# Moving the row sums of the modulation vectors to other gates

## The chip, the cores and the metric

The kernel runs on one core of one Trainium2 chip. The metric is the time of one execution on the device in microseconds (us), as the median of several runs. The kernel before takes 2740.04 us (three runs, 2739.88 to 2740.99).

The engines appear under the short names of the profile: PE is TensorE (matmuls), PEld its weight loads, DVE is VectorE, ACT is ScalarE, POOL is GpSimd, and SP is SyncE, whose queue issues nearly all DMA transfers here. Each engine works through its own list of instructions in a fixed order and waits for the others by semaphores.

## The reference

The reference runs two blocks on 256 tokens of width 1024. Only the first block matters here. It has two trunk layers; layer 0 works on two streams, `lat` and `ctx`, layer 1 on `lat` alone at its end. Each layer begins with modulation vectors, six of width 1024 per stream, from one linear map of a condition:

```python
m_lat = (jax.nn.silu(c) @ w_mod + b_mod)[:, None, :]
m_ctx = jax.nn.silu(c_ctx) @ w_mod + b_mod
sh1, sc1, g1, sh2, sc2, g2 = jnp.split(m_lat, N_MOD, -1)
...
u_lat = h_lat * (1.0 + sc1) + sh1
y_lat, y_ctx = token_mixers(u_lat, u_ctx, ...)
h_lat = layer_norm(DN_ALPHA * h_lat + g1 * y_lat, ln1_g, ln1_b)
u_lat = h_lat * (1.0 + sc2) + sh2
h_lat = layer_norm(DN_ALPHA * h_lat + g2 * expert_choice_ffn(u_lat, ...), ln2_g, ln2_b)
```

The token mixers are four branches (A: global attention, B: Fourier, C: window attention, D: neighbourhood attention). Each branch is multiplied with a matrix and with a gate, a sigmoid of another product of `u`, and the four are added up:

```python
gates = jax.nn.sigmoid(gate_logits)
merged = gates[..., :D_MODEL] * (branches[0] @ w_branch[0])
for i in range(1, N_BRANCH):
    merged = merged + gates[..., i * D_MODEL:(i + 1) * D_MODEL] * (branches[i] @ w_branch[i])
return merged @ w_out
```

## The kernel before

**Matmuls from split weights.** A weight tile of 1 MB (`raw`, 128 x 2048 floats) is loaded by one DMA on SP's queue. Each half of it is split into a high part `wh` on ACT (L257) and a low part `wl` on DVE (L260), and each product is three matmuls (L294 high by high, L295 the one that needs `wl`, L296). `dense_nat` (L298) goes over the tiles of a product and behind each half of a tile calls `pump(1)`.

**Slots.** `raw` tiles take slots in turn: three in the mixers of layer 0, five in those of layer 1. A load waits until the tile that held its slot before, three (five) tiles earlier in the program, has been read.

**Gates.** `gate(i, c)` (L710) handles half `c` of the columns of branch `i`; the text calls it gate 00, 01, 10 and so on. It multiplies `u` with two gate tiles (`wgat`) for every unit of 128 tokens (four units in layer 0, two in layer 1), takes tanh of the result on ACT (`th`), multiplies the split branch (`brs`, split in L272 and L273) with half a branch tile (`wbr`), and combines both on DVE: L737 for branch 0, else L739 into `th`, and an addition into `mg` on POOL (L740; on DVE for the last branch). A gate's products lie in four banks (`acc`) that must be read out before the next ones use them. The order of the steps in the program is written out: `A al ac B F C cl cc 00 01 10 11 D dl dc 20 21 30 31`, where a capital letter is a projection and `al`, `cl`, `dl` (`ac`, ...) are attentions of `lat` (`ctx`). A list scheduler then orders each engine's instructions by priority and its own estimate of when inputs are there; PE fills the wait times of an attention with matmuls of the gate behind it.

**Row sums.** The first third of layer 0's modulation comes from matmuls at the start. The rest, two thirds for layer 0 and three for layer 1, comes from DVE. `mods_rows(l, i, n)` (L486) makes eight steps for a third `i` of layer `l` and `n` streams. A step loads a 1 MB tile of the transposed matrix (`wmt`), and for each half and stream multiplies it with the row of silu(c) (`crow`) and adds up along the row (L497, output `junk` and one column of `mcol`): 2n instructions. The last step of eight adds the bias (L502). They are issued 100 places later in priority, behind the last `wl` split. The steps wait in the list `todo`; `pump(n)` (L507) runs the next n of them, if there are any.

**Who calls pump.** Before each pair of gates, `hook(i)` fills `todo` with the eight steps of one third: (0,1) for two streams with branch 0, (0,2) for two with branch 1, (1,0) for two with branch 2, (1,1) for one with branch 3; in layer 1, (1,2) for one with branch 0. The loop that matters:

```python
                for hi, lo in parts:
...
                    for u, (xh, xl, o) in enumerate(units):
...
                    kg += kp
                    self.pump(1)
```

Of the kernel before, what the change touches and what calls it, by code (L numbers as in the profile page):

```python
# [190 lines left out]
class Net:  # L191
# [99 lines left out]
    def mm3(self, out, xs, ws, first, last):  # L291
        (xh, xl), (wh, wl) = xs, ws
        mm = self.nc.tensor.matmul
        mm(out, lhsT=xh, rhs=wh, start=first, stop=False)  # L294
        mm(out, lhsT=xh, rhs=wl, start=False, stop=False)  # L295
        mm(out, lhsT=xl, rhs=wh, start=False, stop=last)  # L296
# [315 lines left out]
    def mixers(self, mg, gp, pool, l, streams, with_ctx, hook):  # L612
# [16 lines left out]
        nf = len(full)  # L629
# [46 lines left out]
        def who(ss, u):  # L676
            return ss[u // 2], u % 2
# [32 lines left out]
        def gate(i, c):  # L710
            if c == 0:
                hook(i)
            th = {}

            def evac_g(_, u, acc):
                x = gp.tile([128, 512], F32, tag="th", name="th", bufs=(3, 4)[nf - 1])
                th[u] = x
                nc.scalar.activation(x, acc, AF.Tanh, scale=0.5)

            self.dense_nat(us, [[wg[2 * i + c, 0], wg[2 * i + c, 1]]], evac_g)  # L720
            wb = gp.tile([128, 1024], F32, tag="wbr", name="wbr", bufs=1)
            nc.sync.dma_start(wb, I[f"wbr{l}"][i][:, c * 1024:(c + 1) * 1024])
            if c == 0:
                for s in full:
                    brs[s] = self.new_split(gp, 2, 256, "brs" + s)
                    self.split_x(brs[s], br[i, s])
            hi, lo = self.split_w(wb)[0]
            hi, lo = (x.rearrange("p (k n) -> p k n", k=2) for x in (hi, lo))
            for u in range(len(us)):
                s, t = who(full, u)  # L730
                acc = self.bank("acc")
                o = slice(t * 128, (t + 1) * 128)
                for k in range(2):
                    self.mm3(acc, (brs[s][0][:, k, o], brs[s][1][:, k, o]), (hi[:, k], lo[:, k]), k == 0, k == 1)
                m = mg[s, t][:, c * 512:(c + 1) * 512]
                if i == 0:
                    nc.vector.scalar_tensor_tensor(m, th[u], 1.0, acc, op0=OP.add, op1=OP.mult)  # L737
                else:
                    nc.vector.scalar_tensor_tensor(th[u], th[u], 1.0, acc, op0=OP.add, op1=OP.mult)  # L739
                    (nc.gpsimd if i < 3 else nc.vector).tensor_tensor(m, m, th[u], op=OP.add)  # L740
            self.pump(8 if c else 0)


        A = new_mixer()
# [122 lines left out]
        for i in range(4):  # L867
            for c in range(2):
                steps[f"{i}{c}"] = lambda i=i, c=c: gate(i, c)
# [683 lines left out]
    def first(self):  # L1553
# [6 lines left out]
        for l in range(2):  # L1560
            full = names if l == 0 else names[:1]
            post = ExitStack()
            with ExitStack() as sc:
# [27 lines left out]
                    with self.later(400), self.tc.issue_after(self.last_split.ins):  # L1591
                        self.residual(z["lat"], I["ln2_g0"], I["ln2_b0"])

                todo = ([(0, 1, 2)], [(0, 2, 2)], [(1, 0, 2)], [(1, 1, 1)]) if l == 0 else ([(1, 2, 1)], [], [], [])

                def hook(i):
                    self.todo = [f for a in todo[i] for f in self.mods_rows(*a)]

                mr = xsc.enter_context(tc.tile_pool(name="mr", bufs=1))
                n = 2 - l  # L1600
# [9 lines left out]
                with tc.tile_pool(name=f"gate{l}", bufs=1) as gp, tc.tile_pool(name=f"mix{l}", bufs=1) as pool:  # L1610
                    self.ahead = ahead
                    self.mixers(mg, gp, pool, l, xt, l == 0, hook)
# [201 lines left out]
```

## Time and profile before

| what | us |
|---|---|
| median of the timed runs (2739.88 to 2740.99) | 2740.04 |
| the profiled execution, its own time | 2735.72 |
| span of the profiled execution, first to last instruction | 2733.9 |
| TensorE busy in the span | 2431.8 |
| VectorE busy in the span | 1473.5 |
| ScalarE busy in the span | 849.0 |

The mixers of layer 0 run from about 60 to 450 us, their gates from 135 us; then come the output product, the router and the experts of layer 0, and from 1030 us layer 1, whose gates run from about 1090 to 1272 us. A row of the timeline gives the start in us, the duration in us, engine, line, operation, the tiles written and read with their shapes, and a count; in square brackets stands how long the engine was idle just before, and what it waited for. A matmul of the timeline reads as 0.39 us although the next starts 0.23 us later, since they are pipelined. A row of the stage table gives a stretch, its length, and then busy us and number of instructions of PE, PEld, DVE, ACT and POOL, then the granted clock as a share of the full one, the share of the DMA engines and GB/s.

### The profile page before, as it was taken

What the parts mean: (1) busy time and instruction counts of PE and PEld (TensorE: products, weight loads), DVE (VectorE), ACT (ScalarE), POOL (GpSimd) and SP (SyncE); (2) the same over time, 40 slices, a digit from 0 to 9 for tenths busy, and PEclk for the clock granted to TensorE, in tenths of its full rate; (3) what the DMA queues carried; (4) which work ended last, traced back from release to release, by engine and by line L of the source; (5) the groups of instructions that cost most, each with busy time, mean ns of one, the idle gap of its engine ahead of it and who ended that gap; (6) DMA issues with size and microseconds to landing.
All of it is one profiled execution on the core that took longest, in us unless ns stands there. A gap on an engine that the chain in (4) does not pass through costs nothing.

```text
span 2733.9 us, 34804 instructions
## 1 busy us (share of the span) xinstructions
PE 2431.8 (89%) x13994; PEld 1662.4 (61%) x13994; DVE 1473.5 (54%) x2601; ACT 849.0 (31%) x1442; POOL 88.8 (3%) x89
## 2 busy tenths in 40 slices
PE   6999899898898988999856777689999999998998
PEld 3667678552222227668511333369778998877897
DVE  4799896442222238866411212169656755656655
ACT  2443233220000014544100100036454544544543
POOL 0001010000000000010000000000000000000000
PEclk8999999999998899999977877889999999999999
DMA  8146565489999993646899999974264652543650
GB/s 295 37 147 219 157 226 210 152 332 407 421 421 421 422 372 128 225 135 231 333 426 426 426 425 426 426 272 155 93 221 176 253 186 89 193 175 145 234 186 31
DMA packets 116384, 700.83 MB, mean 256 GB/s; under 512 B 26352, under 2 KB 27120, under 8 KB 34688
## 3 DMA queue, kind: packets, MB, share of 16 engines
q1 hardware_dynamic: 114304, 692.33, 65.2%
q0 software_dynamic: 1920, 6.29, 0.6%
q8 instruction: 110, 1.80, 0.3%
q14 instruction: 50, 0.41, 0.0%
HBM read 693.33 MB, written 5.24 MB: 256 GB/s over the span
## 4 chain that ended last, share of the span: by engine, by line
PE 66%; DMA 17%; DVE 11%; ACT 3%; issue 2%; POOL 1%; SPq 0%; DVEq 0%; ACTq 0%; POOLq 0%
PE acc L295 9%; PE acc L296 9%; PE acc L294 9%; PE acc L1018 9%; DMA raw<-in_wgu 6%; PE acc L1050 5%; DMA raw<-in_wdn 3%; PE att L368 2%; PE att L369 2%; DMA raw<-in_xwv 2%; PE att L370 2%; DVE wl L260 2%; PE tp L378 2%; PE att L985 2%; PE acc L369 2%
## 5 line engine op out<-in xcount | busy, mean ns | idle before, releaser
L260 DVE TENSOR_TENSOR wl<-raw,wh 128x1024 fp32r<-128x1024 f32 x384 | 471.0, 1233 | 283.8 <-ACT wh L257 279.0
L257 ACT ACTIVATE wh<-raw 128x1024 fp32r<-128x1024 f32 x384 | 403.7, 1058 | 558.5 <-PE acc L296 258.0
L1018 PE MATMUL acc<-raw,xs 128*64 128x512 f32 (+1 forms) x2048 | 379.1, 647 | 60.6 <-DMA raw<-in_wgu 60.4
L1018 PEld LDWEIGHTS acc<-raw,xs 128*64 128x64 f32 (+1 forms) x2048 | 99.4, 126 | 308.8 <-issue 181.6
L1022 ACT ACTIVATE eth<-acc 64x512 f32<-64x512 f32 x48 | 28.4, 591 | 670.6 <-PE acc L1018 670.6
L1024 DVE SCALAR_TENSOR_TENSOR esg<-eth,acc 64x512 f32<-64x512 f32 x48 | 32.7, 681 | 353.3 <-ACT eth L1022 352.8
L294 PE MATMUL acc<-wh,xtlath 128*128 128x512 f32 (+1 forms) x448 | 177.4, 397 | 8.8 <-ACT wh L257 3.2
L295 PE MATMUL acc<-wl,xtlath 128*128 128x512 f32 (+1 forms) x448 | 176.7, 394 | 2.7 <-DVE wl L260 2.7
L296 PE MATMUL acc<-wh,xtlatl 128*128 128x512 f32 (+1 forms) x448 | 175.9, 393 | 0.0
L497 DVE SCALAR_TENSOR_TENSOR junk<-raw,crow 128x1024 bf16<-128x1024 f32 x128 | 162.2, 1267 | 8.6 <-DMA raw<-in_wmt 7.2
L1050 PE MATMUL acc<-raw,eaT 128*64 128x512 f32 x512 | 140.2, 710 | 10.3 <-DVE eaT L207 5.5
L368 PE MATMUL att<-xth,wh 128*128 128x256 f32 x512 | 146.2, 286 | 2.9 <-DVE xth L288 2.9
L369 PE MATMUL att<-xth,wl 128*128 128x256 f32 x512 | 146.0, 285 | 0.0
L370 PE MATMUL att<-xtl,wh 128*128 128x256 f32 x512 | 145.8, 285 | 0.0
L368 PE MATMUL acc<-xth,wh 128*128 128x256 f32 x416 | 120.3, 289 | 4.5 <-DVE xth L288 4.5
L369 PE MATMUL acc<-xth,wl 128*128 128x256 f32 x416 | 120.0, 289 | 0.0
L370 PE MATMUL acc<-xtl,wh 128*128 128x256 f32 x416 | 119.4, 287 | 0.0
L294 PEld LDWEIGHTS acc<-wh,xtlath 128*128 128x128 f32 x448 | 85.5, 191 | 29.0 <-ACT wh L257 3.8
L1061 DVE TENSOR_TENSOR eylat<-acc,g2lat 32x512 f32<-32x512 f32 x32 | 21.9, 684 | 150.3 <-PE acc L1050 150.1
L294 PE MATMUL acc<-wh,xtctxh 128*128 128x512 f32 (+1 forms) x272 | 101.8, 375 | 1.0 <-DVE th L739 1.0
L368 PEld LDWEIGHTS att<-xth,wh 128*128 128x128 f32 x512 | 99.5, 194 | 3.8 <-issue 3.2
L294 PE MATMUL acc<-wh,hidh 128*128 128x512 f32 x256 | 101.3, 396 | 0.0
(535 smaller groups left out, 4844.7 us busy)
## 6 DMA issues: line engine op xcount, KB each, us to landing
raw<-in_wgu SPq DMA_DIRECT2D x256, 1024.0 KB, 19.5
raw<-in_wdn SPq DMA_DIRECT2D x128, 1024.0 KB, 19.0
raw<-in_w SPq DMA_DIRECT2D x64, 1024.0 KB, 4.8
raw<-in_wmt SPq DMA_DIRECT2D x40, 1024.0 KB, 4.9
raw<-in_wgat SPq DMA_DIRECT2D x32, 1024.0 KB, 4.8
raw<-in_wmod SPq DMA_DIRECT2D x8, 1024.0 KB, 7.5
raw<-in_wqkv SPq DMA_DIRECT2D x8, 1024.0 KB, 10.7
wbr<-in_wbr SPq DMA_DIRECT2D x16, 512.0 KB, 4.8
```

What stands on the lines that cost most here:

```text
L257: self.nc.scalar.activation(hi, s, AF.Copy)
L260: self.last_lo = self.nc.vector.tensor_tensor(lo, s, hi.bitcast(F32), op=OP.subtract)
L294: mm(out, lhsT=xh, rhs=wh, start=first, stop=False)
L295: mm(out, lhsT=xh, rhs=wl, start=False, stop=False)
L296: mm(out, lhsT=xl, rhs=wh, start=False, stop=last)
L368: mm(acc[:, b], lhsT=h[:, s], rhs=xh[:, k], start=k == 0, stop=False)
L369: mm(acc[:, b], lhsT=l[:, s], rhs=xh[:, k], start=False, stop=False)
L370: mm(acc[:, b], lhsT=h[:, s], rhs=xl[:, k], start=False, stop=k == 7)
L378: self.nc.tensor.transpose(t[:, j], src[:, (b + j) * 128:(b + j + 1) * 128], self.ident)
L497: nc.vector.scalar_tensor_tensor(junk, r[:, b * 1024:b * 1024 + 1024], 1.0, self.crow[:, s], op0=OP.mult, op1=OP.mult, accum_out=self.mcol ...
L1018: nc.tensor.matmul(o, lhsT=lt, rhs=w[:, a, c], start=k == 0, stop=k == 7)
L1050: nc.tensor.matmul(yb[64 * h:64 * h + 64], lhsT=aT[:, kf], rhs=w[:, f, h * 512:(h + 1) * 512], start=kf == 0, stop=kf == 7)
```

## The change

The last line of `gate` and the filling of `todo` are edited. All thirds of a layer go into `todo` at once, at the first gate: three in layer 0, two in layer 1. The third (1,1) moves from layer 0 to layer 1. The last line of a gate now runs `nf - 1` steps (`nf` is the number of streams, 2 in layer 0 and 1 in layer 1), and at the very last gate whatever is left.

```diff
-            self.pump(8 if c else 0)
+            self.pump(len(self.todo) if i == 3 and c else nf - 1)
...
-                todo = ([(0, 1, 2)], [(0, 2, 2)], [(1, 0, 2)], [(1, 1, 1)]) if l == 0 else ([(1, 2, 1)], [], [], [])
+                todo = ((0, 1, 2), (0, 2, 2), (1, 0, 2)) if l == 0 else ((1, 1, 1), (1, 2, 1))
...
                 def hook(i):
-                    self.todo = [f for a in todo[i] for f in self.mods_rows(*a)]
+                    if i == 0:
+                        self.todo = [f for a in todo for f in self.mods_rows(*a)]
```

The first place is DVE's queue in layer 0 at the start of gate 10. Numbers behind names only tell tiles apart. Before, from the branch tile's split of gate 01 (`wl_1866`) to the two splits of gate 10's first tile (`wl_1908`, `wl_1912`):

```order
L260 TENSOR_TENSOR wl_1866<-wbr_1863,wh_1865 128x1024
L497 SCALAR_TENSOR_TENSOR junk_1777,mcol0_83<-raw_1775,crow_226 128x1024 x4
L260 TENSOR_TENSOR wl_1908<-raw_1905,wh_1907 128x1024
L497 SCALAR_TENSOR_TENSOR junk_1818,mcol0_83<-raw_1816,crow_226 128x1024 x4
L737 SCALAR_TENSOR_TENSOR mg_152<-th_1855,acc_1869 128x512
L737 SCALAR_TENSOR_TENSOR mg_153<-th_1857,acc_1877 128x512
L260 TENSOR_TENSOR wl_1912<-raw_1905,wh_1911 128x1024
```

In the changed kernel the same two splits are `wl_1922` and `wl_1926`:

```order
L737 SCALAR_TENSOR_TENSOR mg_155<-th_1868,acc_1900 128x512
L497 SCALAR_TENSOR_TENSOR junk_1825,mcol0_83<-raw_1823,crow_226 128x1024
L273 TENSOR_TENSOR brslatl_2074<-br_972,brslath_2073 128x512
L497 SCALAR_TENSOR_TENSOR junk_1825,mcol0_83<-raw_1823,crow_226 128x1024
L273 TENSOR_TENSOR brsctxl_2078<-br_991,brsctxh_2077 128x512
L502 TENSOR_TENSOR mcol0_83<-mcol0_83,bmodt_81 128x32
L497 SCALAR_TENSOR_TENSOR junk_1857,mcol0_83<-raw_1855,crow_226 128x1024 x4
L497 SCALAR_TENSOR_TENSOR junk_1910,mcol0_83<-raw_1908,crow_226 128x1024
L260 TENSOR_TENSOR wl_1922<-raw_1919,wh_1921 128x1024
L260 TENSOR_TENSOR wl_1926<-raw_1919,wh_1925 128x1024
```

Counted from the start of the program, 24 row sums stood ahead of the first of these splits before, and 37 stand ahead of it now. They also stood on either side of the last combinations of gate 01 (`mg`), and now stand behind them.

The second place is DVE's queue in layer 0 at the projection D. Before, the end of the gate's row sums and the splits of D's second tile (`raw_2368`):

```order
L497 SCALAR_TENSOR_TENSOR junk_2219,mcol0_83<-raw_2217,crow_226 128x1024
L273 TENSOR_TENSOR brslatl_2979<-br_1166,brslath_2978 128x512
L497 SCALAR_TENSOR_TENSOR junk_2219,mcol0_83<-raw_2217,crow_226 128x1024
L273 TENSOR_TENSOR brsctxl_2983<-br_1351,brsctxh_2982 128x512
L497 SCALAR_TENSOR_TENSOR junk_2250,mcol0_83<-raw_2248,crow_226 128x1024 x4
L502 TENSOR_TENSOR mcol0_83<-mcol0_83,bmodt_81 128x32
L260 TENSOR_TENSOR wl_2371<-raw_2368,wh_2370 128x1024
L260 TENSOR_TENSOR wl_2375<-raw_2368,wh_2374 128x1024
```

In the changed kernel, the splits of both of D's tiles (`raw_2338` and `raw_2396`):

```order
L497 SCALAR_TENSOR_TENSOR junk_2272,mcol1_84<-raw_2270,crow_226 128x1024
L273 TENSOR_TENSOR brslatl_3008<-br_1166,brslath_3007 128x512
L497 SCALAR_TENSOR_TENSOR junk_2272,mcol1_84<-raw_2270,crow_226 128x1024
L273 TENSOR_TENSOR brsctxl_3012<-br_1351,brsctxh_3011 128x512
L497 SCALAR_TENSOR_TENSOR junk_2272,mcol1_84<-raw_2270,crow_226 128x1024 x2
L260 TENSOR_TENSOR wl_2341<-raw_2338,wh_2340 128x1024
L260 TENSOR_TENSOR wl_2345<-raw_2338,wh_2344 128x1024
L497 SCALAR_TENSOR_TENSOR junk_2329,mcol1_84<-raw_2327,crow_226 128x1024 x4
L260 TENSOR_TENSOR wl_2399<-raw_2396,wh_2398 128x1024
L260 TENSOR_TENSOR wl_2403<-raw_2396,wh_2402 128x1024
```

Before, the splits of D's first tile stood behind 53 and 57 row sums and those of the second behind 64. Now both splits of the first stand behind 76, and those of the second behind 80.

The third place is DVE's queue in layer 1, in gate 01. Before, the splits of its two gate tiles (`raw_7602`, `raw_7636`):

```order
L260 TENSOR_TENSOR wl_7605<-raw_7602,wh_7604 128x1024
L207 COPY PT_7272<-tp_7347 128x4x128
L260 TENSOR_TENSOR wl_7609<-raw_7602,wh_7608 128x1024
L260 TENSOR_TENSOR wl_7639<-raw_7636,wh_7638 128x1024
L273 TENSOR_TENSOR brslatl_7677<-br_7003,brslath_7676 128x512
L497 SCALAR_TENSOR_TENSOR junk_7553,mcol1_84<-raw_7551,crow_6478 128x1024
L1639 TENSOR_SCALAR resg_8622<-g_8580 128x8
L1639 TENSOR_SCALAR resb_8623<-b_8582 128x8
L497 SCALAR_TENSOR_TENSOR junk_7570,mcol1_84<-raw_7568,crow_6478 128x1024
L260 TENSOR_TENSOR wl_7643<-raw_7636,wh_7642 128x1024
```

In the changed kernel these tiles are `raw_7561` and `raw_7605`:

```order
L260 TENSOR_TENSOR wl_7568<-raw_7561,wh_7567 128x1024
L497 SCALAR_TENSOR_TENSOR junk_7512,mcol1_84<-raw_7510,crow_6437 128x1024
L273 TENSOR_TENSOR brslatl_7656<-br_6962,brslath_7655 128x512
L497 SCALAR_TENSOR_TENSOR junk_7529,mcol1_84<-raw_7527,crow_6437 128x1024
L1640 TENSOR_SCALAR resg_8622<-g_8580 128x8
L1640 TENSOR_SCALAR resb_8623<-b_8582 128x8
L497 SCALAR_TENSOR_TENSOR junk_7529,mcol1_84<-raw_7527,crow_6437 128x1024
L502 TENSOR_TENSOR mcol1_84<-mcol1_84,bmodt_81 128x16
L497 SCALAR_TENSOR_TENSOR junk_7585,mcol1_84<-raw_7583,crow_6437 128x1024 x2
L497 SCALAR_TENSOR_TENSOR junk_7602,mcol1_84<-raw_7600,crow_6437 128x1024 x2
L260 TENSOR_TENSOR wl_7608<-raw_7605,wh_7607 128x1024
L260 TENSOR_TENSOR wl_7612<-raw_7605,wh_7611 128x1024
```

The split that directly followed the first tile's pair now has seven row sums ahead of it. PE's order stays that of before except for a few places where matmuls that need only `wh` are put ahead of those that need `wl`, at the start of gates.

## Rows read from the trace of the kernel before

**Rows 1.** The page's first part: busy us, share of the span, instructions.

```profile
PE 2431.8 (89%) x13994; PEld 1662.4 (61%) x13994; DVE 1473.5 (54%) x2601; ACT 849.0 (31%) x1442; POOL 88.8 (3%) x89
```

**Rows 2.** The stage table of three stretches.

```profile
core 0: us, PE busy (x) PEld busy (x) DVE busy (x) ACT busy (x) POOL busy (x), PEclk, DMA share, GB/s
...
190.00:290.00 100.00, 94.17 (x411) 75.55 (x410) 94.59 (x139) 26.79 (x34) 15.83 (x8) 0.99 0.60 215
290.00:450.00 160.00, 152.77 (x709) 115.81 (x707) 132.24 (x258) 53.10 (x99) 11.56 (x8) 0.98 0.65 226
...
1147.00:1190.00 43.00, 43.00 (x215) 35.66 (x214) 27.76 (x34) 17.16 (x20) 8.36 (x4) 1.00 0.59 220
```

**Rows 3.** Timeline of PE in layer 0, gate 10 to D.

```profile
214.97 0.39 PE L295 MATMUL acc<-wl,xtlath 128*128 128x512 f32 x1
...
271.00 0.50 PE L294 MATMUL acc<-wh,xtlath 128*128 128x512 f32 x1 [1.70 <-DVE th L739]
...
286.61 0.73 PE L294 MATMUL acc<-wh,xtlath 128*128 128x512 f32 x2 [3.18 <-ACT wh L257]
...
287.87 0.69 PE L295 MATMUL acc<-wl,xtlath 128*128 128x512 f32 x1 [0.30 <-DVE wl L260]
...
288.78 0.63 PE L294 MATMUL acc<-wh,xtlath 128*128 128x512 f32 x1
289.21 0.63 PE L295 MATMUL acc<-wl,xtlath 128*128 128x512 f32 x1
...
291.61 0.39 PE L296 MATMUL acc<-wh,xtlatl 128*128 128x512 f32 x1
...
299.55 0.39 PE L296 MATMUL acc<-wh,xtctxl 128*128 128x512 f32 x1
```

**Rows 4.** The row sums' line, 60 to 500 us: shortest, median, longest in ns.

```profile
L497 DVE SCALAR_TENSOR_TENSOR junk<-raw,crow x112: 1204/1220/2348, 135.1 to 439.7; 128x1024 bf16<-128x1024 f32 x112
```

**Rows 5.** Timeline of DVE in layer 0, gate 10 to D.

```profile
227.51 1.22 DVE L260 TENSOR_TENSOR wl<-wbr,wh 128x1024 fp32r<-128x1024 f32 x1
...
243.65 1.27 DVE L739 SCALAR_TENSOR_TENSOR th<-th,acc 128x512 f32<-128x512 f32 x2
244.84 2.35 DVE L497 SCALAR_TENSOR_TENSOR junk<-raw,crow 128x1024 bf16<-128x1024 f32 x1
...
255.31 1.23 DVE L497 SCALAR_TENSOR_TENSOR junk<-raw,crow 128x1024 bf16<-128x1024 f32 x1
...
256.58 1.22 DVE L497 SCALAR_TENSOR_TENSOR junk<-raw,crow 128x1024 bf16<-128x1024 f32 x1
...
280.55 0.68 DVE L273 TENSOR_TENSOR brsctxl<-br,brsctxh 128x512 fp32r<-128x512 f32 x1
```

**Rows 6.** DMA issues, 190 to 300 us: count, size, median us to landing.

```profile
raw<-in_wmt SPq DMA_DIRECT2D x13, 1024.0 KB, 4.9
```

**Rows 7.** Waits of SP's queue, 60 to 520 us: total, times, longest.

```profile
SPq L235 <- DVE wl L260: 108.3, 19, 14.3
SPq L235 <- DVE junk L497: 86.2, 22, 8.1
```

**Rows 8.** Timeline of PE in layer 0, behind D's attention.

```profile
362.58 0.41 PE L378 MATMUL tp<-constt,P 128*128 128x128 f32 x2 [0.87 <-DVE P L582]
...
395.72 0.50 PE L294 MATMUL acc<-wh,xtctxh 128*128 128x512 f32 x1 [0.41 <-DVE th L739]
...
404.46 0.50 PE L295 MATMUL acc<-wl,xtlath 128*128 128x512 f32 x1 [1.42 <-DVE wl L260]
```

**Rows 9.** Timeline of DVE in layer 1, gate 01.

```profile
1146.75 2.35 DVE L260 TENSOR_TENSOR wl<-raw,wh 128x1024 fp32r<-128x1024 f32 x2
```

**Rows 10.** Timeline of PE in layer 1: gate 01's second tile, then D.

```profile
1153.74 0.39 PE L295 MATMUL acc<-wl,xtlath 128*128 128x512 f32 x1
...
1175.51 0.39 PE L295 MATMUL acc<-wl,xtlath 128*128 128x512 f32 x1
```

## The prediction

> **What bounds the kernel now.** I read the first part of the page, then the stage table, and last the timelines of VectorE and TensorE around the gates. Over the whole span TensorE is busy 89% and VectorE 54% [rows 1], which looks like a TensorE kernel with VectorE to spare. The stage table says otherwise for the part that the change touches. From 190 to 290 us (gates 01, 10 and 11 of the first layer and the start of the projection D) TensorE is busy 94.17 us of 100 and VectorE 94.59; from 290 to 450 us they are 152.77 and 132.24 of 160; in layer 1, from 1147 to 1190 us, TensorE is busy all 43 us and VectorE only 27.76 [rows 2]. The timeline of TensorE shows that VectorE loses the race in the first of these stretches: at 271.00 us a matmul waits 1.70 us for a gate's product to be taken out of its bank, at 286.61 us TensorE waits 3.18 us for the second tile of D, and then 0.30 us for its low half [rows 3]. What fills VectorE there is row sums: 112 of them before 500 us, 1.22 us each in the median [rows 4]. Back to back they start 1.27 us apart (255.31, 256.58) [rows 5].
>
> **What the change really moves.** `dense_nat` pumps one step behind each half of a weight tile, so a gate with two tiles already does four steps in its loop. Before, the eight steps of a pair of gates are all done there, and the last line of `gate` finds nothing left. Now that line adds one step per gate in the first layer (`nf - 1` is 1): five steps in each of gates 00, 01, 10 and 11, the remaining four in gate 20, none in 21, 30 and 31. That is no even pace of three. In layer 1 `nf - 1` is 0: four steps in each of gates 00 to 11 and none later. Over the program nothing is added or removed: 128 row sums, 40 loads of 1 MB, the same matmuls in nearly the same order. What moves, at four row sums per step in layer 0: 80 instead of 64 stand ahead of D's second tile (16 more), and 16 instead of 48 behind it (32 fewer). Layer 1 gets 32 instead of 16, all ahead of its D. The loads go along: 20 tiles of 1 MB ahead of D instead of 16. Each lands 4.9 us after issue [rows 6]. There are three slots in layer 0, and a gate's first tile now takes its slot from a row-sum tile of the gate before, where it took it from a gate tile. SP's queue already waits 86.2 us for row sums to free a slot and 108.3 us for splits [rows 7]. The bias additions move too, one small instruction per vector, and I cost them at nothing.
>
> **Term 1, layer 0 up to the end of D.** VectorE runs its queue in order, so I walk it with 1.27 us a row sum, 1.22 a split, 0.64 a `th` product and 0.68 a `brs` split [rows 5]. A gate is 120 matmuls at 0.227 us = 27.2, D is 96 = 21.8 (291.61 to 299.55 is 35 steps [rows 3]).
> Gate 10: before, the split of gate 10's branch tile starts at 227.51 [rows 5], behind 35 row sums and behind the four splits of gate 10's weight tiles. In the new order the first of these four splits stands behind 37 row sums (it stood behind 24). So it starts at 227.51 + 2 x 1.27 - 4 x 1.22 = 225.2 and ends at 226.4. TensorE wanted it at 214.97 [rows 3]: it waits 11.4. The queue puts row sums that nobody waits for ahead of a split that TensorE waits for.
> Gate 11: TensorE is ready at 226.4 + 27.2 = 253.6. VectorE has 18 row sums (22.9), five splits (6.1) and four `th` products (2.6) to do until the first split is there, and 2.2 more because two row sums run beside GpSimd's additions, where one took 2.35 instead of 1.22 [rows 5]: 260.2, a wait of 6.6.
> D: TensorE is ready at 287.4. VectorE has 21 row sums (26.7), five splits (6.1), `th` (2.6), `brs` (1.4) and 2.2 beside GpSimd: 299.2, a wait of 11.8. After such a wait the clock is at its lower level, 1.2 GHz, for a while: behind the 3.18 us of before, matmuls take 0.63 instead of 0.39 and start 0.43 instead of 0.23 apart until 291.61 [rows 3], some ten of them, 2.0 us. D ends at 299.2 + 21.8 + 2.0 = 323.0; before, its last matmul started at 299.55. That is +23. Counting sums alone, 16 x 1.27 = 20.3, less up to 3 for loads that VectorE waits for now and that would be there, gives 17 as the lower end. The upper end is 28, if one gate tile also waits the 4.9 us of a load that a late row sum held back. I take 22, between the plain count and the walk.
>
> **Term 2, layer 0 behind D.** Gate 20 has four steps before and after, so the attention of D with its waits for bias tables stays. Behind it 32 row sums, 40.6 us of VectorE, are gone. That gives back only what TensorE waited for there: 0.87, 0.41 and 1.42 us [rows 8]. I take -3, with 0 and -7 as ends (all idle time of that stretch is 160 - 152.77 = 7.2 [rows 2], most of it in the attention). The rest of the 40.6 us was hidden by TensorE's own work and pays nothing.
>
> **Term 3, layer 1.** Until the pair of splits at 1146.75 [rows 9] both orders agree. The first split of gate 01's second tile was the other one of that pair; now it comes behind seven more row sums and a `brs` split: 1147.9 + 8.9 + 0.7 + 1.2 = 1158.7. TensorE wants it at 1153.74 [rows 10] and waits 5.0. Gate 10 then starts at 1158.7 + 36 x 0.227 = 1166.9, and its first split is there by 1166.2. Its second tile comes behind eight row sums, two `th` and 2.2 beside GpSimd, with five splits up to its own (10.2 + 1.3 + 2.2 + 6.1): 1178.5, where TensorE is ready at 1172.3. The branch tile comes behind another split and four sums, at 1186.0, where TensorE is ready at 1183.9. Waits of 5.0, 6.2 and 2.1, and about 1 for a slow clock: D, which started at 1175.51 [rows 10], starts 14.3 late. Ends: 16 x 1.27 = 20.3 less the 15.2 that VectorE idles in the stretch [rows 2] is 5; with none of the idle time used it is 20. I take 13, just under the walk, since some of the idle time may be of use.
>
> **Sum.** 22 - 3 + 13 = +32. The profiled execution took 2735.7 us (its span is 2733.9), and would take 2767.7. The median of the timed runs before is 2740.0, 4.3 above it, so on that scale the forecast is 2772. The rest of the program keeps its order, and both expert phases start only when the mixers are through, so nothing pays this back.
>
> **Two rules against this reading.** The stage table puts VectorE at 94.59 of 100 us where the page has 54% [rows 1, 2]. The Trainium skill, "Perfetto Trace Analysis", section Identifying the Most-Contended Engine, works on the engine with the highest occupancy. Read over the whole span, that rule names TensorE, and row sums that move on VectorE would be free: rival 2 below. The stage rows disagree with that reading.
> One wait of 3.18 us was followed by one slow stretch that cost 2.0 us [rows 3]. The Trainium skill, "TensorE: Matmul & The Clock Gate", section HAM oscillation, says that long waits re-throttle the clock each time, and that the penalty is half of the throttled time. By it each of the five long waits above would cost 2.0, 10 in all against my 3, and the sum would be +39. I count only those in front of D, because inside the gates TensorE waits for VectorE's queue anyway.
>
> **Rivals.**
> 1. Layer 1 swallows its share: VectorE idles 15.2 us of 43 there [rows 2]. Against it: that idle time lies behind the splits that TensorE waits for, not ahead of them. Then 2740 + 22 - 3 = 2759. Chance 0.15.
> 2. The row sums are hidden altogether: they are issued at a lower priority. Against it: a queue doesn't reorder, and 13 more sums stand ahead of gate 10's first split. 2740. Chance 0.06.
> 3. Faster: the freed stretch behind D decides. Its price is all of the 7.2 us that TensorE idles there [rows 2], and it decides if VectorE's lead at gate 01 covers all but a few of the 16 sums in front. Then 2733. Against it: the lead is used up at 271.00 already [rows 3]. Chance 0.05.
> 4. Slots: the first tiles of gates 01, 10, 11 and of D are each loaded 4.9 us late [rows 6], because their slots come free only behind row sums. 32 + 4 x 4.9 = 51.6, so 2792. For it: 86.2 us of SP's waits are of this kind [rows 7]. Against it: by the walk the load fits into the time that the split waits in its queue. Chance 0.06.
> The forecast, slower in both layers, has 0.68.
>
> **How the numbers follow.** 0.2%, 5.5 us, is about what a measurement of this kernel can tell from no change. Rival 3 is faster by 7 us: 0.05. Rival 2 is no change: 0.06. The forecast and rivals 1 and 4 are slower: 0.89. The ends of the terms add up to 17 - 7 + 5 = +15 and 28 - 0 + 20 = +48; I set 2755 to 2787, which holds the forecast and rival 1 and leaves out rivals 2 to 4 (0.17).
>
> **What the new profile would show.** Right: TensorE waits for a split at the start of gate 10 (about 11 us), of gate 11 (about 7) and of D (about 12); D in layer 0 ends near 323; VectorE is busy almost without a break from 212 to 307; gates 21, 30 and 31 hold no row sum, with VectorE well below its present load; in layer 1 there are waits in gates 01 and 10 and at the branch tile, and D starts later. Term 1 is wrong if D ends less than 12 us late, term 3 if layer 1's mixers take no longer than before, and the whole forecast if the stretch from 190 to 290 us shows TensorE as busy as now.

## The result, and the profile after

The kernel after takes 2773.14 us (median of four runs, 2766.44 to 2778.65), the kernel before 2740.04. The ratio is 1.0122, with a 95% interval of 1.0107 to 1.0138: slower by 33.1 us, where 32 were forecast (2772.0, 2755 to 2787). Its profiled execution took 2774.02 us, with a span of 2772.2.

The stage table of the kernel after, for the stretches of [rows 2]. Layer 1's first branch product starts 25.9 us later than before, so its stretch is moved by as much:

```profile
core 0: us, PE busy (x) PEld busy (x) DVE busy (x) ACT busy (x) POOL busy (x), PEclk, DMA share, GB/s
190.00:290.00 100.00, 83.97 (x354) 66.52 (x353) 95.97 (x146) 23.70 (x31) 11.58 (x7) 0.93 0.63 226
290.00:450.00 160.00, 146.16 (x664) 110.36 (x665) 103.96 (x207) 50.16 (x93) 16.18 (x10) 0.95 0.48 160
1172.90:1215.90 43.00, 33.97 (x143) 25.49 (x143) 40.98 (x62) 14.06 (x17) 7.46 (x4) 0.96 0.93 356
```

From 190 to 290 us TensorE lost ten of its hundred us (94.17 before, 83.97 now), while VectorE stayed full. Behind that stretch VectorE has 28 us less to do (132.24 before, 103.96 now). In layer 1 VectorE went from 27.76 busy us to 40.98, and TensorE, which was busy all 43 us, now idles nine of them (33.97 busy). The work moved forward in time, from where nobody waited for VectorE to where TensorE does.

The timeline of TensorE in layer 0 of the kernel after, for [rows 3] (start us, length, engine, line, operation, tiles, shapes, count, idle before and its releaser):

```profile
225.52 1.22 PE L294 MATMUL acc<-wh,xtlath 128*128 128x512 f32 x2 [10.44 <-ACT wh L257]
...
257.18 0.74 PE L294 MATMUL acc<-wh,xtlath 128*128 128x512 f32 x2 [2.31 <-ACT wh L257]
...
259.92 0.79 PE L295 MATMUL acc<-wl,xtlath 128*128 128x512 f32 x1 [1.12 <-DVE wl L260]
...
296.93 1.22 PE L294 MATMUL acc<-wh,xtlath 128*128 128x512 f32 x2 [8.90 <-ACT wh L257]
...
300.09 0.79 PE L295 MATMUL acc<-wl,xtlath 128*128 128x512 f32 x1 [1.51 <-DVE wl L260]
...
322.99 0.39 PE L296 MATMUL acc<-wh,xtctxl 128*128 128x512 f32 x1
```

Three waits that were not there: at gate 10 (10.44 us), at gate 11 (2.31, and 1.12 for the low half) and at D (8.90 and 1.51). D's last product, at 299.55 before, starts at 322.99. What TensorE waits for at gate 10 is seen in the rows of VectorE, SP and ScalarE around it:

```profile
218.31 1.22 DVE L497 SCALAR_TENSOR_TENSOR junk<-raw,crow 128x1024 bf16<-128x1024 f32 x1
...
219.57 0.33 SPq L235 DMA_DIRECT2D raw<-in_wgat  x1
...
224.41 2.01 ACT L257 ACTIVATE wh<-raw 128x1024 fp32r<-128x1024 f32 x2 [8.89 <-DMA raw<-in_wgat]
...
225.23 1.22 DVE L497 SCALAR_TENSOR_TENSOR junk<-raw,crow 128x1024 bf16<-128x1024 f32 x1
...
226.38 2.35 DVE L260 TENSOR_TENSOR wl<-raw,wh 128x1024 fp32r<-128x1024 f32 x2
```

A row sum on VectorE ends at about 219.5 and frees its slot. At 219.57 SP issues the load of gate 10's first weights into it; 4.8 us later, at 224.41, ScalarE makes the high halves. VectorE is all the while at more row sums, and makes the low halves at 226.38. So two things come last at nearly the same time: the load that had to wait for a slot, and the split that had to wait for VectorE. The trace alone doesn't tell which of them is the cause; the experiments do.

Layer 1 of the kernel after, TensorE up to D (for [rows 10]). The names of two gates need a correction here. TensorE's products with the branches of gates 00, 01, 10 and 11 start at 1117.03, 1140.52, 1158.96 and 1172.56 in the trace of before, ahead of D at 1175.51. So what the change's third place, [rows 9], [rows 10] and the prediction call gates 01 and 10 of layer 1 are its gates 10 and 11. The walk goes by these rows and not by the names, so its sum stays. In the kernel after, gate 10's second tile comes first here, then gate 11's second tile and branch tile, and D:

```profile
1183.58 0.74 PE L294 MATMUL acc<-wh,xtlath 128*128 128x512 f32 x2 [4.02 <-ACT wh L257]
...
1184.84 0.79 PE L295 MATMUL acc<-wl,xtlath 128*128 128x512 f32 x1 [0.52 <-DVE wl L260]
...
1203.21 0.50 PE L295 MATMUL acc<-wl,xtlath 128*128 128x512 f32 x1 [2.89 <-DVE wl L260]
...
1210.65 0.50 PE L295 MATMUL acc<-wl,brslath 128*128 128x512 f32 x1 [1.11 <-DVE wl L260]
...
1213.99 0.50 PE L295 MATMUL acc<-wl,xtlath 128*128 128x512 f32 x1 [0.20 <-DVE wl L260]
```

D starts at 1213.99, 38.5 us later than before. Layer 1's first branch product started 25.9 later (1142.90 against 1117.03), so 12.6 of it are layer 1's own.

### The profile page after: what moved, and what is told of

Its sections match the earlier page's. It is cut to its first block, busy times and chain, and to the rows that moved or that the text cites. A ratio compares the mean times of both kernels' runs of the same rounds, so it can differ in the third digit from the quotient of the medians.

```text
span 2772.2 us, 34818 instructions
## 1 busy us (share of the span) xinstructions
PE 2449.0 (88%) x13994; PEld 1672.4 (60%) x13994; DVE 1474.8 (53%) x2601; ACT 847.8 (31%) x1442; POOL 89.7 (3%) x89
## 4 chain that ended last, share of the span: by engine, by line
PE 64%; DMA 18%; DVE 12%; ACT 3%; issue 2%; POOL 1%; SPq 0%; DVEq 0%; POOLq 0%; ACTq 0%
PE acc L295 9%; PE acc L296 9%; PE acc L294 9%; PE acc L1018 9%; DMA raw<-in_wgu 7%; PE acc L1050 5%; DMA raw<-in_wdn 3%; DVE wl L260 3%; PE att L368 2%; PE att L369 2%; PE att L370 2%; DMA raw<-in_xwv 2%; PE tp L378 2%; PE acc L369 1%; DMA raw<-in_xwk 1%
## 5 line engine op out<-in xcount | busy, mean ns | idle before, releaser
L1061 DVE TENSOR_TENSOR eylat<-acc,g2lat 32x512 f32<-32x512 f32 x32 | 21.9, 685 | 154.9 <-PE acc L1050 154.7
L295 PEld LDWEIGHTS acc<-wl,xtlath 128*128 128x128 f32 x448 | 87.3, 195 | 26.9 <-DVE wl L260 10.9
L1050 PEld LDWEIGHTS acc<-raw,eaT 128*64 128x64 f32 x512 | 42.2, 167 | 101.3 <-issue 88.3
```

The source lines that it names most:

```text
L1050: nc.tensor.matmul(yb[64 * h:64 * h + 64], lhsT=aT[:, kf], rhs=w[:, f, h * 512:(h + 1) * 512], start=kf == 0, stop=kf == 7)
```

## The experiments

In this table "ahead" is the number of row sums that stand on VectorE ahead of the first weight split of gate 10, of gate 11 and of D in layer 0, counted in the order in which each built program's instructions stand on the engine. Times are medians.

| kernel | us | ahead of gate 10, gate 11, D |
|---|---|---|
| before | 2740 | 24, 39, 53 |
| after | 2773.14 | 37, 55, 76 |
| layer 1 of the change alone | 2752.41 | 24, 39, 53 |
| layer 0 of the change alone | 2762.26 | 37, 55, 76 |
| layer 0 with six steps per gate | 2779.10 | 45, 69, 93 |
| three steps per gate, two in layer 1 | 2725.36 | 24, 36, 48 |
| after, row sums of half length | 2733.80 | 40, 59, 80 (halves) |
| after, without the loads | 2737.24 | 24, 39, 55 |
| after, loads kept but unread | 2742.19 | 24, 39, 55 |
| the same, splits held behind the sums | 2777.74 | 40, 60, 80 |

**Each layer by itself.** First layer 1 of the change alone:

```diff
-            self.pump(len(self.todo) if i == 3 and c else nf - 1)
+            self.pump(0)
```

> Layer 0 goes back to four steps of row sums per gate (its three thirds in the first six gates, none in the last two); layer 1 is that of the changed kernel (two thirds, four steps per gate). If the cost is the length of VectorE's queue ahead of mixer D in each layer by itself, layer 0 is within 1 us of the kernel before up to gate 11 and gains 2 to 4 us in D, whose gates now hold no row sums, and layer 1 loses its 12.6 us: 2740 + 12.6 - 3 = 2750 us (2747 to 2754). If the 4.6 us that the changed kernel lost among layer 0's experts belong to layer 0's shift they are absent here; if they belong to something else in the change (layer 1's rows, code layout) they stay and the time is 2754 to 2758. If layer 1's waits arose only because layer 0 came late, the time is 2737 to 2740.

Measured: 2752.41 us, ratio 1.0049 (1.0037 to 1.0061), +12.2. Layer 1's waits are those of the kernel after, 20 us earlier in the span (4.02 us at 1163.48, 2.89 at 1183.05), and that part came as expected. Layer 0 did not gain its 2 to 4 us: its last output product starts at 502.67, against 502.55 in the first profile of before and 503.69 in the second. In the first profile of before it starts 203.00 us after D's last product, here 203.16, although gates 30 and 31 hold no row sums any more. Then layer 0 alone:

```diff
-            self.pump(len(self.todo) if i == 3 and c else nf - 1)
+            self.pump(nf - 1 if i < 3 else 0)
...
+                    elif l == 0 and i == 3:
+                        self.todo = self.mods_rows(1, 1, 1)
```

> Layer 0 as in the changed kernel up to gate 21 (5, 5, 5, 5, 4 steps), and the third (1, 1) back in gates 30 and 31 as before; layer 1 as before. By the theory of VectorE's queue the first low product of D is 23 us later than before (11 of it at gate 10, 6 or 7 at gate 11, the rest at D), the waits within D stay (no 2 to 3 us back), and layer 1 is unchanged: 2740 + 23 = 2763 us (2760 to 2769, the upper end if the 4.6 us among the experts come with it). If the loss is due to layer 1 swallowing or to both layers together, it is under 2755.

Measured: 2762.26 us, ratio 1.0077 (1.0065 to 1.0089), +22.1. The two runs add up to +34.3, the whole change costs +33.1: the layers don't share a cause that would count twice, and neither swallows its share.

**More of it.** Layer 0 with six steps per gate, from the run before:

```diff
-            self.pump(nf - 1 if i < 3 else 0)
+            self.pump(2 * nf - 2 if i < 3 else 0)
```

> Layer 0 alone with six steps per gate instead of five (24 steps in the gates of 00 to 11, none behind), layer 1 as before. If each row sum that is moved ahead of D costs its own length, the four steps more (16 row sums at 1.20 us) make D end 19 to 22 us later than in the run with layer 0 alone, less 0 to 3 us that come back in gate 20: 2762 + 18 = 2780 us (2775 to 2787). If the cost is bounded (by the slots, or by the number of thirds, that is the same) the time stays at 2760 to 2768.

Measured: 2779.10 us, ratio 1.0144 (1.0127 to 1.0161), 16.8 more than with five steps, where row sums of 16 x 1.22 = 19.5 us were moved. The summary of TensorE's waits from 186 to 330 us (in total, times, longest), of this kernel:

```profile
PE acc L294 <- ACT wh L257: 29.9, 3, 10.3
PE tp L378 <- DVE sst L580: 2.9, 1, 2.9
PE acc L295 <- DVE wl L260: 2.5, 2, 1.5
PE tp L378 <- DVE P L582: 2.1, 1, 2.1
PE tp L592 <- DVE PT L207: 0.8, 1, 0.8
```

Its stage row:

```profile
core 0: us, PE busy (x) PEld busy (x) DVE busy (x) ACT busy (x) POOL busy (x), PEclk, DMA share, GB/s
190.00:290.00 100.00, 75.73 (x301) 59.48 (x300) 97.43 (x149) 20.99 (x26) 7.84 (x4) 0.83 0.63 224
```

In the run with layer 0 alone the waits for `wh` and `wl` come to 22.5 and 2.7 us, and only 0.2 us are of another kind. So 12.8 of the 16.8 us are waits: 7.2 more for splits, and 5.8 in the attention ahead of gate 01, where TensorE now waits for VectorE's small steps (`sst`, `P`, `PT`). The granted clock from 190 to 290 us is 0.83 here and 0.95 there; I take the rest to be TensorE's slower work behind the waits, which no run isolates. Each row sum that is moved ahead costs 1.05 us, nearly its own length.

**A pace that is even.** Three steps per gate in layer 0 and two in layer 1:

```diff
+            self.todo, self.rest = self.rest[:1 + nf], self.rest[1 + nf:]
...
-            self.pump(len(self.todo) if i == 3 and c else nf - 1)
+            self.pump(0)
...
-                        self.todo = [f for a in todo for f in self.mods_rows(*a)]
+                        self.rest = [f for a in todo for f in self.mods_rows(*a)]
```

> An even pace: three steps per gate in layer 0 (three thirds over eight gates), two per gate in layer 1 (two thirds over eight gates). By the theory of VectorE's queue 15 or 16 row-sum steps fewer stand ahead of D in layer 0 than in the changed kernel (and fewer than before, by four), so that the waits at gates 10 and 11 are shorter than before's and D starts 5 to 15 us earlier than before's 271.34; behind D VectorE has room, so layer 0 ends 2 to 12 us earlier than before; layer 1 has 8 steps ahead of D as before, spread over four gates, and is within 2 us of before. 2740 - 2 to 12: 2733 us (2728 to 2740). If the number of thirds in a layer is what costs, or the load slots that they share with the gates' weights, it is 2755 or more in spite of the pace.

Measured: 2725.36 us (2723.74 to 2735.01), ratio 0.9949 (0.9934 to 0.9964): faster than both kernels, and 14.8 us under before, more than expected. The stage table, for [rows 2]:

```profile
core 0: us, PE busy (x) PEld busy (x) DVE busy (x) ACT busy (x) POOL busy (x), PEclk, DMA share, GB/s
190.00:290.00 100.00, 100.00 (x446) 81.88 (x446) 80.14 (x115) 29.64 (x41) 14.75 (x8) 1.00 0.52 184
290.00:450.00 160.00, 153.83 (x732) 117.18 (x732) 136.68 (x272) 56.65 (x107) 14.88 (x8) 0.98 0.56 193
```

TensorE is busy all 100 us, with VectorE at 80.14; VectorE's work is spread into the stretch behind D, where it is 136.68 busy of 160 and holds nobody up. I had the place of the gain wrong: D doesn't start earlier, since TensorE hardly waited ahead of it before. The waits within D [rows 3] are gone, and those in gates 20 and 21 [rows 8]: D's last product starts at 291.87 instead of 299.55, the last output product of layer 0 at 493.68 instead of 502.55. These are 8.9 of the 14.8 us. From the first branch product of layer 1 to the fold's first product (the first one behind the last gate) it is 154.7 us, against 155.1 before. The profiled execution took 2731.26 us, 5.9 more than the median of its kernel, so where the other us were gained is not shown.

**Shorter row sums.** In the kernel after, half of each sum's columns are left out:

```diff
-                        nc.vector.scalar_tensor_tensor(junk, r[:, b * 1024:b * 1024 + 1024], 1.0, self.crow[:, s],
+                        nc.vector.scalar_tensor_tensor(junk[:, :512], r[:, b * 1024:b * 1024 + 512], 1.0, self.crow[:, s, :512],
```

> The changed kernel with each row sum over the first 512 of its 1024 columns (half of each sum is left out); same order, same loads, same slots, same count of instructions. If VectorE's time is what D waits for, a row sum of about 0.65 us instead of 1.20 takes 0.55 x 64 = 35 us off VectorE's queue in the stretch to D, and the waits at gates 10, 11 and D go in both layers: 2735 us (2728 to 2743). If the load slots or the DMA queues hold the gates' weights back, the waits stay: 2762 us or more.

Measured: 2733.80 us, ratio 0.9978 (0.9968 to 0.9988). The whole loss is gone, with the loads and their slots unchanged. By count the splits stand further back than in the kernel after (80 ahead of D). But a half sum takes 0.69 us at the median, so 80 of them take 55 us, as long as 45 whole ones, and before there were 53 whole ones. So it is the time ahead of a split that costs, not the number of sums. By itself this spoke for VectorE's time.

**No loads.** In the kernel after, the row sums read a resident vector, and their loads are left out:

```diff
-            r = self.raw(self.I[f"wmt{l}"][i - 1 + l, k])
...
-                        nc.vector.scalar_tensor_tensor(junk, r[:, b * 1024:b * 1024 + 1024], 1.0, self.crow[:, s],
+                        nc.vector.scalar_tensor_tensor(junk, self.crow[:, 0], 1.0, self.crow[:, s],
```

> The changed kernel with the row sums reading a resident vector instead of their loaded rows (the loads of the modulation rows in both layers are left out, and with them their use of the load slots; the sums are of other numbers); as many row sums of the same shape at the same places of VectorE's queue. If VectorE's time is what D waits for, the waits at gates 10, 11 and D stay within some us of the changed kernel's and move from ScalarE's split (which waited for a load) to VectorE's: 2768 us (2755 to 2778). If the loads' slots or the DMA queues hold the gates' weights back, the waits go: 2736 to 2745 us. A time between says how much of the wait was the slots.

Measured: 2737.24 us, ratio 0.9986 (0.9977 to 0.9995). Here my theory as I had put it fell: as many row sums of the same length, and no loss. The stage table of this kernel:

```profile
core 0: us, PE busy (x) PEld busy (x) DVE busy (x) ACT busy (x) POOL busy (x), PEclk, DMA share, GB/s
190.00:290.00 100.00, 96.67 (x428) 78.31 (x427) 98.97 (x150) 28.40 (x38) 17.79 (x8) 1.00 0.26 90
290.00:450.00 160.00, 153.32 (x706) 115.34 (x704) 108.39 (x222) 53.14 (x98) 12.03 (x8) 0.98 0.34 114
```

VectorE is fuller than in the kernel after (98.97 us of 100), and still TensorE is busy 96.67. So a full VectorE by itself does not cost. But my expectation had one thing wrong: the row sums don't stand at the same places. Without the loads the list scheduler puts gate 10's first split behind 24 row sums and not 37 (table above), and D's last split behind 64, as before, and not 80: the sums that the change had put ahead of D stand behind it again. Two explanations remain: the slots and DMA queues, or the places.

**Loads kept, unread.** The same with the loads (the first minus line above is undone):

> The changed kernel with its loads of the modulation rows kept, while the row sums read the resident vector (so the rows are loaded and not used; the sums are of other numbers). A slot is then free again as soon as its load has landed, and no longer when VectorE has come to its row sums; the bytes moved and the order of the loads' issue are those of the changed kernel. If what held the weights back is the slot that a row sum keeps until VectorE reaches it, the waits go as without loads: 2738 us (2733 to 2748). If it is the traffic of these loads on the DMA queue ahead of the weights, they stay: 2762 us or more.

Measured: 2742.19 us, ratio 1.0003 (0.9993 to 1.0013): the waits are gone although 1 MB after 1 MB is still loaded. From 190 to 290 us:

```profile
core 0: us, PE busy (x) PEld busy (x) DVE busy (x) ACT busy (x) POOL busy (x), PEclk, DMA share, GB/s
190.00:290.00 100.00, 95.99 (x424) 77.39 (x423) 98.25 (x146) 27.86 (x35) 17.83 (x8) 1.00 0.52 187
```

The traffic of the loads is ruled out: the same loads run here (187 GB/s in the stretch, 90 without the loads) and nothing is lost. The places are again 24, 39 and 55, so slots and places are not told apart yet.

**Free slots, held splits.** The run with unread loads, with one more constraint:

```diff
-        self.behind = []
+        self.behind, self.last_row = [], None
...
-            first = self.behind.pop(0) if self.behind else None
+            first = self.behind.pop(0) if self.behind else self.last_row
+            self.last_row = None
...
-                        nc.vector.scalar_tensor_tensor(junk, self.crow[:, 0], 1.0, self.crow[:, s],
+                        self.last_row = nc.vector.scalar_tensor_tensor(junk, self.crow[:, 0], 1.0, self.crow[:, s],
```

> The run with unread loads (row sums of the resident vector, loads kept), with one addition: each weight tile's first split is held on VectorE behind the row sums of the steps before it. In the run with unread loads 24 row sums stand ahead of gate 10's first split on VectorE, as in the kernel before; in the changed kernel it is 37, here 40, at gate 11 60 and 60, at D 76 and 80. If what D and the gates wait for is the place of the splits in VectorE's queue, and the slots cost only by forcing that place, the waits come back though the slots are free: 2776 us (2765 to 2788). If the slot that a load waits for in the run is itself the cost, free slots keep the time at 2740 to 2750 in whatever order.

Measured: 2777.74 us, against 2743.39 for the kernel before beside it, ratio 1.0126 (1.0109 to 1.0143). With the row tiles' slots free the loss is back in full. Gate 10's first tile is early: ScalarE makes its high half at 214.00, and VectorE comes to the low half at 228.64. Its second tile is issued at 231.02 and landed at 238.91, but there TensorE waits only 0.45 us, at 243.17. TensorE's waits for splits are now named after VectorE's own (the first at gate 10, at gate 11 and at D; below them the two largest sums from 190 to 330 us, in total, times, longest):

```profile
229.91 0.50 PE L296 MATMUL acc<-wl,xtlath 128*128 128x512 f32 x1 [1.79 <-DVE wl L261]
...
266.58 0.79 PE L296 MATMUL acc<-wl,xtlath 128*128 128x512 f32 x1 [3.31 <-DVE wl L261]
...
302.40 0.80 PE L296 MATMUL acc<-wl,xtlath 128*128 128x512 f32 x1 [3.31 <-DVE wl L261]
...
PE acc L296 <- DVE wl L261: 11.5, 7, 3.3
PE acc L295 <- DVE th L740: 3.5, 2, 1.8
```

Its stage row:

```profile
core 0: us, PE busy (x) PEld busy (x) DVE busy (x) ACT busy (x) POOL busy (x), PEclk, DMA share, GB/s
190.00:290.00 100.00, 87.07 (x350) 67.90 (x349) 98.03 (x152) 23.33 (x32) 6.95 (x4) 0.93 0.47 168
```

TensorE does 350 matmuls in that stretch, 354 in the kernel after and 424 with unread loads. So the place of the splits in VectorE's queue alone is enough for a loss of this size. It is not wait for wait the loss of the kernel after, since the held order is stricter: three to five more row sums stand ahead (table), gate 00 already ends late (its last product starts at 190.20, in the kernel after at 185.32), and TensorE also waits for banks to be read out (`th`). Layer 0's last output product starts at 528.03, 4.2 us later than in the kernel after, and layer 1 takes 168.0 us where it took 167.7.

I read it so that the slots cost by way of that place: gate 10's weights are loaded into a slot that a row sum has just left (219.57 above), and a split whose weights can't be there yet is not put ahead of that row sum. The run with unread loads differs from the kernel after only in what the row sums read, and has the splits first again; that this is the scheduler's reason is argued, not shown.

**Fewer slots.** Layer 1 has five load slots and layer 0 three. With three in layer 1, before and after:

```diff
-                xsc.enter_context(self.more_raw(2 * l))
+                xsc.enter_context(self.more_raw(0))
```

> The kernel before with three load slots in layer 1's gates instead of five (layer 0 has three); it is the control for the next run. By either theory layer 1's gates grow by little, as its 16 row sums ahead of D leave VectorE room: 155 us from the first branch product to the first product of the fold become 155 to 162, and the time 2740 to 2748.

> The changed kernel with three load slots in layer 1's gates instead of five. If a gate's weights wait for a slot that a row sum holds, the change costs layer 1 more than the 12.6 us that it costs with five: 18 to 30 us over the control. If VectorE's time alone is the cause, it costs 12 to 13 over the control as before, since VectorE's work is the same.

Measured: 2739.69 us (ratio 1.0002, 0.9992 to 1.0011) and 2782.57 (1.0155, 1.0140 to 1.0170). From the first branch product of layer 1 to the fold's first product it is 158.0 us (1122.73 to 1280.68) and 175.6 (1144.74 to 1320.32): the change costs layer 1 17.6 us with three slots, 12.6 with five (155.1 before, 167.7 after). That is more than VectorE's time alone allows and a little less than I expected of the slots. It fits the forced order: VectorE does the branch tile's split of layer 1's gate 10 behind 24 row sums with three slots and behind 20 with five, while before it is 16 with either. With one profile of each this is not proof.

**The stretch that the prediction left out.** The profile of the kernel after is 38.3 us longer than that of before, the medians differ by 33.1. Of the 38.3, 4.6 arise between the two layers' gates, a stretch of over 600 us that holds layer 0's router and experts and the start of layer 1, and that the change doesn't touch. The kernel before, profiled twice more:

> The kernel before, profiled once more, for the 4.6 us that the changed kernel's profile shows among layer 0's experts. From the end of layer 0's last attention product to layer 1's first branch product the profile of before has 614.1 us, those of the five other kernels 618.6 to 623.4. If that stretch differs from execution to execution whatever the kernel, this profile has 617 to 624 us there and the execution takes 2738 to 2746; if the change lengthens it, it has 614 again.

> The same kernel, profiled a third time, for the spread of that stretch: 613 to 624 us if it differs from execution to execution, and the two layers' gates within 1 us of those of the first profile.

Measured: 2742.06 and 2743.60 us. The stretch from layer 0's last output product to layer 1's first branch product, in the first profile of before and in the second:

```profile
core 0: us, PE busy (x) PEld busy (x) DVE busy (x) ACT busy (x) POOL busy (x), PEclk, DMA share, GB/s
502.94:1117.03 614.09, 544.53 (x2522) 239.44 (x2521) 239.75 (x475) 93.14 (x184) 10.36 (x12) 0.92 0.86 348
```

```profile
504.08:1123.07 618.99, 549.42 (x2523) 241.43 (x2521) 239.76 (x475) 93.03 (x184) 10.36 (x12) 0.91 0.86 345
```

It took 614.1 us the first time and 619.0 and 618.0 in the later two; the kernel after has 618.7 there. The 4.6 us were not the change's: the first profile of before was a quick one (2735.72 us, 4.3 under its median).

## Why the prediction was right

- **Term 1, +22 (walk +23).** D's last product starts at 322.99, 23.4 us later than 299.55 [rows 3]; the walk said 323.0. Its steps hold too, within 1.3 us: the first low products of gates 10 and 11 and of D start at 227.65, 259.92 and 300.09, where the walk had the splits ready at 226.4, 260.2 and 299.2. TensorE's idle times are shorter than the forecast 11.4, 6.6 and 11.8 us: 10.44 at gate 10, 3.4 (2.31 and 1.12) at gate 11 and 10.4 (8.90 and 1.51) at D. Part of each wait is filled with the few products that need only the high half, at a slow clock (1.22 us for two of them at 225.52; the granted clock from 190 to 290 us is 0.93, where it was 0.99 [rows 2]), and what TensorE loses there it need not wait for the split, since VectorE's queue sets the time. Most of the wait is filed under ScalarE's split, not under VectorE's as forecast, because the load came late too.
- **Term 2, -3.** Layer 0's last output product starts at 523.86 instead of 502.55, 21.3 late, so 2.1 came back. That the freed VectorE gave it back is not shown. From D's last product to the last output product the three profiles of before take 203.00, 204.17 and 204.94 us, the kernel after takes 200.87, and the run with layer 1 alone, without row sums in gates 30 and 31, takes 203.16. The term is small, as forecast, and about as large as that spread.
- **Term 3, +13.** 12.6 in the profile, 12.2 in the run with layer 1 alone. The waits were forecast as 5.0, 6.2 and 2.1 us and 1 for a slow clock. TensorE idles 4.5, 2.9 and 1.4 us at these places and 0.2 at D, 9.0 in all; the other 3.6 us are slower products (granted clock 0.96 in the stretch, before 1.00). So the total is right and its parts are shifted from waiting to slow work.
- **Sum.** 23.4 - 2.1 + 12.6 = 33.9; the medians say 33.1, the forecast 32.
- **What was only half right: the reason.** The prediction has a queue that puts row sums ahead of a split that TensorE waits for, and that is what the held splits show. But its first paragraph and its plain count take VectorE's fullness and 16 more row sums for the cost. The run with unread loads has the same row sums on a VectorE as full, and loses nothing, because the splits stand first. The prediction could use the places, since the order of the changed program shows them, without knowing why they are there.
- **Rival 4, slots** (2792). Its price, 4.9 us of a load on top of each wait, didn't come. What the prediction held against it is what the rows show: the load fits into the time that the split waits in its queue (224.41 against 226.38). As the reason for the order, the slots were there all the same.
- **Rivals 1 to 3.** Layer 1 swallowed nothing (12.6). Nothing was hidden: the lower priority of the row sums did not keep the splits first (37 row sums ahead of gate 10 instead of 24). What came back behind D, 2.1 us, is far from the 7.2 of rival 3.
- **The rule of slow clocks.** The Trainium skill, "TensorE: Matmul & The Clock Gate", section HAM oscillation, says that long waits re-throttle the clock each time and that half of the throttled time is lost. The rows agree that the clock falls with long waits: behind 10.44 and 8.90 us of idle time two products took 1.22 us, behind 2.31 us 0.74, and the granted clock of the stretch fell from 0.99 to 0.93. Added up over the five waits it would have made +39; the medians say 33.1. In layer 0 the slow products of gate 11 (0.79 us at 259.92) cost nothing of their own, since D's first low product starts at 300.09, when its split is there. In layer 1 they cost more than the 1 us that the prediction allowed.

Left open: whether a fourth slot in layer 0 would have kept the splits first at five steps per gate. It wasn't tried.

## What to carry to other kernels

Filler work on an in-order engine is not free just because the engine has time for it; it is free if nothing on the path stands behind it in the queue. In this kernel, where the filler's data and the path's data take turns in the same few slots, the order of the loads is the order of the work, so the pace of the filler (three steps per gate and not five) decides how far the path's work is pushed back. Add up the time of what stands ahead of the waiting instruction in each version, and don't go by the engine's busy share.

## What the runs showed of the hardware that was not expected

- VectorE at 98.97 us of 100 went with a TensorE at 96.67 (no loads), and VectorE at 95.97 with a TensorE at 83.97 (after): a full engine in front of another says little about how long the other waits.
- The stretch with the router and experts of layer 0 and the start of layer 1, with the same instructions, took 614.1, 619.0 and 618.0 us in three profiles of one kernel, with 348 GB/s and a granted clock of 0.92 in the quick one and 345 and 0.91 in the second. That is as much as the smallest effects looked for here, so two profiles are compared stage by stage, and their totals by medians.
